# Weighted sum of two expert outputs: the first load in one piece, and the zeroes made by ScalarE

## The chip, the cores and the metric

The kernel runs on one core of one Trainium2 chip. The metric is the device time of one execution in microseconds; the median of three runs of the kernel before is 238.86 us (238.84 to 238.90).

## The reference

```python
expert_outputs   # (16, 1024, 2, 512) float32
combine_weights  # (16, 1024, 2)      float32
weights = combine_weights[..., np.newaxis]
return np.sum(expert_outputs * weights, axis=2).astype(np.float32)   # (16, 1024, 512)
```

There are 16 x 1024 = 16,384 tokens. Each has two expert outputs of 512 numbers and two weights; the output is the weighted sum of the two. The input is twice as large as the output.

## The kernel before

**Layout.** The tokens are spread over 128 partitions, 128 tokens to a partition. One token's input, both experts, is 4 KB (`k * h` = 1024 floats). The first 115 tokens of a partition (`main`) come from one part of the input, the last 13 (`LAST`) from another, so that the last tile has rows of its own. `TILES` (line 32) cuts the 128 tokens into ten tiles of 12 or 13; a tile of 13 is 13 x 4 KB = 52 KB in each partition.

**Rooms.** The buffer `et` (line 62) has four rooms (`ROOM`, line 29) of 13, 13, 12 and 13 tokens. Tile g goes into room g mod 4. A tile is combined in place, and its result, half as large, is stored out of the same room (the last tile's result goes into room 0, by `FREE`). So the load of tile g + 4 has to wait for the store of tile g.

**The work of one tile** (`combine`, line 81). For tiles 0 to 7 VectorE multiplies the whole tile by its weights (line 88) and adds the two halves (line 97). Tile 8 is shared between ScalarE (line 92) and VectorE (lines 94 to 97). For tile 9 ScalarE multiplies one half of each token (line 102), and VectorE multiplies the other and adds (line 103), token by token.

**Queues.** Loads are issued by SyncE (line 76), and so are the last two stores (line 130: tiles 7 and 8 together, and tile 9). All other stores, and the weights, are issued by ScalarE. The order on each engine is the order of the program; nothing reorders it. An instruction that waits holds up what stands behind it on its engine.

**The start.** VectorE clears `zt`, a tile of 16 x 128 floats (line 108). ScalarE then issues its first four DMAs: `zt` to 16 places of the output (line 111; 8 KB, which the true results overwrite later; the first store waits for it), the weights of the first 115 tokens of each partition (line 112, through line 79; 128 rows of 920 bytes into `wt`), and the weights of the last 13 in two halves (line 114). After these, an activation of one column (line 115, into `warm`) has ScalarE load its activation table. SyncE meanwhile issues five loads (lines 118 and 119): `FIRST` (line 33) splits tile 0 into 2 and 11 tokens, and the 2 are moved in pieces of at most 4 KB (`max_dma_last_dim`), one token each; the 11 and the tiles 1, 2 and 3 go as one row of 44, 52, 48 and 52 KB for each partition.

**Counters.** Each DMA counts up a semaphore when it lands. There are eight of them, given out by the framework, so DMAs share them, and one that takes a counter over waits until the DMA that had it has landed.

Of the kernel before, what the change touches and what calls it, by code (L numbers as in the profile page):

```python
# [1 line left out]

# [4 lines left out]


@with_exitstack
def kernel(  # L10
    ctx: ExitStack,
    tc: tile.TileContext,
    expert_outputs: bass.AP,
    combine_weights: bass.AP,
    out: bass.AP,
):

    nc = tc.nc
    b, s, k, h = expert_outputs.shape
    assert k == 2
    n = b * s
    P = nc.NUM_PARTITIONS
    per = n // P
    assert per * P == n

    ROOM = [13, 13, 12, 13]
    ROOMS = len(ROOM)  # L30
    SITE = [sum(ROOM[:i]) for i in range(ROOMS)]
    TILES = [13, 13, 12, 13, 13, 13, 12, 13, 13, 13]
    FIRST = [2, 11, 13, 12, 13]
    STORES = [[0], [1], [2], [3], [4], [5], [6], [7, 8], [9]]
    WHOLE = [0, 1, 2, 3, 4, 5, 6, 7]
    MIXED = [8]
    ALONE = 3
    FREE = {9: 0}
    LAST = 13
    assert all(c <= ROOM[g % ROOMS] for g, c in enumerate(TILES))  # L40
    assert sum(TILES) == per and [g for st in STORES for g in st] == list(range(len(TILES)))
    main = per - LAST
    starts = [sum(TILES[:g]) for g in range(len(TILES))]

    def rows(x):

        first = x[0 : P * main, :].rearrange("(p t) f -> p t f", p=P)
        second = x[P * main : n, :].rearrange("(p t) f -> p t f", p=P)
        return lambda t, c: first[:, t : t + c, :] if t < main else second[:, t - main : t - main + c, :]

    flat = out.rearrange("b s h -> (b s) h")
    eo = rows(expert_outputs.rearrange("b s k h -> (b s) (k h)"))
    cw = rows(combine_weights.rearrange("b s k -> (b s) k"))
    o = rows(flat)

    dt = mybir.dt.float32
    mult = mybir.AluOpType.mult
    add = mybir.AluOpType.add
    copy = mybir.ActivationFunctionType.Copy

    pool = ctx.enter_context(tc.tile_pool(name="all", bufs=1))
    et = pool.tile([P, sum(ROOM), k * h], dt)
    halves = et.rearrange("p j (k h) -> p (j k) h", k=k)
    wt = pool.tile([P, per * k], dt)
    wk = wt.rearrange("p (t k) -> p t k", k=k)
    zt = pool.tile([16, 128], dt)
    warm = pool.tile([P, 1], dt)

    def place(t):
        g = max(g for g in range(len(TILES)) if starts[g] <= t)  # L70
        return SITE[g % ROOMS] + t - starts[g]

    def load(t, c, **kw):
        at = place(t)
        assert place(t + c - 1) == at + c - 1
        nc.sync.dma_start(out=et[:, at : at + c], in_=eo(t, c), **kw)  # L76

    def weights(q, t, c):
        q.dma_start(out=wk[:, t : t + c, :], in_=cw(t, c))

    def combine(g, base):
        at, c, t0 = SITE[g % ROOMS], TILES[g], starts[g]
        if g in WHOLE or g in MIXED:
            room = halves[:, k * at : k * (at + c), :]
            x0, x1 = et[:, at : at + c, 0:h], et[:, at : at + c, h : 2 * h]
            if g in WHOLE:
                wb = wt[:, k * t0 : k * (t0 + c)].unsqueeze(2).to_broadcast([P, k * c, h])
                nc.vector.tensor_tensor(out=room, in0=room, in1=wb, op=mult)  # L88
            else:
                for i in range(ALONE, c):  # L90
                    x = et[:, at + i, 0:h]
                    nc.scalar.activation(out=x, in_=x, func=copy, scale=wt[:, k * (t0 + i) : k * (t0 + i) + 1])  # L92
                w1 = wk[:, t0 : t0 + c, 1:2].to_broadcast([P, c, h])
                nc.vector.tensor_tensor(out=x1, in0=x1, in1=w1, op=mult)  # L94
                w0 = wk[:, t0 : t0 + ALONE, 0:1].to_broadcast([P, ALONE, h])
                nc.vector.tensor_tensor(out=x0[:, 0:ALONE], in0=x0[:, 0:ALONE], in1=w0, op=mult)  # L96
            nc.vector.tensor_tensor(out=halves[:, base : base + c, :], in0=x0, in1=x1, op=add)  # L97
            return
        for i in range(c):
            t = k * (t0 + i)  # L100
            x0, x1 = halves[:, k * (at + i), :], halves[:, k * (at + i) + 1, :]
            nc.scalar.activation(out=x0, in_=x0, func=copy, scale=wt[:, t : t + 1])  # L102
            nc.vector.scalar_tensor_tensor(  # L103
                out=halves[:, base + i, :], in0=x1, scalar=wt[:, t + 1 : t + 2], in1=x0, op0=mult, op1=add
            )

    with tc.manual_schedule():
        nc.vector.memset(zt, 0.0)  # L108

        ahead = flat[0 : P * main, :].rearrange("(q t) h -> q (t h)", q=16)  # L110
        nc.scalar.dma_start(out=ahead[:, 0:128], in_=zt)  # L111
        weights(nc.scalar, 0, main)
        for half in (slice(0, P // 2), slice(P // 2, P)):
            nc.scalar.dma_start(out=wk[half, main:per, :], in_=cw(main, per - main)[half])
        nc.scalar.activation(out=warm, in_=nc.const_aps.tensor(1.0, (P, 1), dt), func=copy)  # L115

        t = 0
        for i, c in enumerate(FIRST):
            load(t, c, **({"max_dma_last_dim": k * h * 4} if i == 0 else {}))
            t += c  # L120
        assert t == sum(TILES[:ROOMS])
        for j, st in enumerate(STORES):
            room = FREE.get(st[0], st[0] % ROOMS)
            base, c = SITE[room] * k, 0
            for g in st:
                combine(g, base + c)
                c += TILES[g]
            assert c <= k * ROOM[room]
            q = nc.sync if j in (7, 8) else nc.scalar
            q.dma_start(out=o(starts[st[0]], c), in_=halves[:, base : base + c, :])  # L130
            for g in st:
                if g + ROOMS < len(TILES):
                    load(starts[g + ROOMS], TILES[g + ROOMS])


# [1 line left out]
_INS = ['expert_outputs', 'combine_weights']  # L137
_OUTS = [((16, 1024, 512), 'float32')]


# [23 lines left out]
```

## Time and profile before

| what | value |
|---|---|
| median of three runs | 238.86 us |
| span of the profiled execution, first to last instruction | 237.1 us |
| VectorE busy | 190.0 us |
| ScalarE busy | 15.8 us |
| moved by DMA | 100.80 MB (67.24 read, 33.56 written) |
| mean rate over the span | 425 GB/s |

The profile is of one execution. It gives that execution's span and not its device time; the difference of the span to the median of the runs is 1.76 us. Times in the rows are microseconds from the start of the span, durations marked ns are nanoseconds. Each row of the timeline has its start, its length, the engine, the line of the kernel, the operation, the tile written and read, and in brackets the idle time before it and what ended that idle time. An engine name that ends in q (SPq, ACTq) is the engine's instruction queue issuing a DMA; the rows of DMA issues give the size of each DMA and the median time from issue to landing. The rows of stages give a stretch of time, its length, the busy time of VectorE (DVE), ScalarE (ACT) and GpSimd (POOL) with the number of instructions that touch it, the granted clock of the matmul engine, which this kernel doesn't use, then the mean share of the 16 DMA engines that is busy, and the rate.

### The profile page before, as it was taken

How to read it: one execution, taken by the hardware profiler on the slowest of the kernel's cores; microseconds unless marked ns; L12 is line 12 of the kernel's file. 1: busy time of each engine (PE TensorE's matmuls, PEld its weight loads, DVE VectorE, ACT ScalarE, POOL GpSimd, SP SyncE). 2: the span in 40 equal slices, each digit the busy share in tenths (PEclk: the TensorE clock that was granted, in tenths of full speed). 3: DMA queues.
4: the chain of work that ended last, by engine and by line, in shares of the span. 5: the costliest groups of instructions: out<-in, count | busy, mean ns of one | idle time of the engine just before them, and what ended most of it. 6: DMA issues, size and time to landing. Idle time of an engine off the chain costs nothing.

```text
span 237.1 us, 154 instructions
## 1 busy us (share of the span) xinstructions
DVE 190.0 (80%) x33; ACT 15.8 (7%) x25; POOL 0.2 (0%) x4
## 2 busy tenths in 40 slices
DVE  0006999999999999999999998998499969919400
ACT  2000000000000000000000000000000055019200
POOL 0000000000000000000000000000000000000000
DMA  8999999989999999999899999999899999899996
GB/s 300 388 481 434 432 421 398 470 348 485 449 431 458 431 440 390 486 420 420 359 492 409 409 509 392 431 503 431 359 431 503 420 397 483 381 431 431 431 431 287
DMA packets 3344, 100.80 MB, mean 425 GB/s; under 512 B 512, under 2 KB 656, under 8 KB 912
## 3 DMA queue, kind: packets, MB, share of 16 engines
q1 hardware_dynamic: 2000, 77.33, 75.9%
q10 hardware_dynamic: 1344, 23.47, 23.0%
HBM read 67.24 MB, written 33.56 MB: 425 GB/s over the span
## 4 chain that ended last, share of the span: by engine, by line
DVE 55%; DMA 36%; issue 1%; ACT 0%; DVEq 0%; ACTq 0%; SPq 0%
DVE et L88 35%; DVE et L97 17%; DMA out_dram<-et 17%; DMA et<-in_expert_outputs_dram 12%; DMA wt<-in_combine_weights_dram 8%; DVE et L103 3%; ACT et L102 0%; DVEq L159 0%; ACTq L111 0%; DVE zt L108 0%; DVEq L88 0%; SPq L76 0%; ACTq L102 0%
## 5 line engine op out<-in xcount | busy, mean ns | idle before, releaser
L88 DVE TENSOR_TENSOR et<-et,wt 128x13312 f32<-128x13312 f32 (+1 forms) x8 | 110.0, 13754 | 23.8 <-DMA wt<-in_combine_weights_dram 18.7
L97 DVE TENSOR_TENSOR et<-et 128x6656 f32<-128x6656 f32 (+1 forms) x9 | 62.8, 6973 | 0.4
L92 ACT ACTIVATE et<-et,wt 128x512 f32<-128x512 f32 x10 | 6.2, 708 | 188.0 <-DMA et<-in_expert_outputs_dram 188.0
L103 DVE SCALAR_TENSOR_TENSOR et<-et,wt 128x512 f32<-128x512 f32 x13 | 8.7, 747 | 5.0 <-ACT et L102 5.0
L102 ACT ACTIVATE et<-et,wt 128x512 f32<-128x512 f32 x13 | 8.1, 707 | 14.0 <-DMA et<-in_expert_outputs_dram 14.0
L94 DVE TENSOR_TENSOR et<-et,wt 128x6656 f32<-128x6656 f32 x1 | 7.1, 7093 | 2.3 <-DMA et<-in_expert_outputs_dram 2.3
L96 DVE TENSOR_TENSOR et<-et,wt 128x1536 f32<-128x1536 f32 x1 | 1.8, 1751 | 0.0
L115 ACT ACT_TABLE_LOAD x1 | 1.3, 1283 | 3.1 <-issue 3.1
L108 DVE MEMSET zt<- 16x128 f32 x1 | 0.2, 165 | 0.8 <-PEq L148 0.8
L115 ACT ACTIVATE warm<-const-float32-1.0 128x1 f32<-128x1 f32 x1 | 0.2, 203 | 0.0
L148 POOL MEMSET const-bfloat16-1.0<- 128x1 bf16 x1 | 0.1, 102 | 0.0
L148 POOL MEMSET const-uint8-127<- 128x1 uint8 x1 | 0.1, 101 | 0.0
L148 POOL MEMSET const-float32-0.0<- 128x1 f32 x1 | 0.1, 99 | 0.2 <-issue 0.2
L148 POOL MEMSET const-float32-1.0<- 128x1 f32 x1 | 0.1, 98 | 0.0
## 6 DMA issues: line engine op xcount, KB each, us to landing
et<-in_expert_outputs_dram SPq DMA_DIRECT2D x7, 6656.0 KB, 32.2
out_dram<-et ACTq DMA_DIRECT2D x5, 3328.0 KB, 34.7
et<-in_expert_outputs_dram SPq DMA_DIRECT2D x2, 6144.0 KB, 41.1
out_dram<-et SPq DMA_DIRECT2D x1, 6656.0 KB, 19.9
out_dram<-et ACTq DMA_DIRECT2D x2, 3072.0 KB, 37.2
et<-in_expert_outputs_dram SPq DMA_DIRECT2D x1, 5632.0 KB, 18.2
out_dram<-et SPq DMA_DIRECT2D x1, 3328.0 KB, 14.0
et<-in_expert_outputs_dram SPq DMA_DIRECT2D x1, 1024.0 KB, 5.0
```

Source lines behind the costliest of these rows:

```text
L88: nc.vector.tensor_tensor(out=room, in0=room, in1=wb, op=mult)
L92: nc.scalar.activation(out=x, in_=x, func=copy, scale=wt[:, k * (t0 + i) : k * (t0 + i) + 1])
L94: nc.vector.tensor_tensor(out=x1, in0=x1, in1=w1, op=mult)
L96: nc.vector.tensor_tensor(out=x0[:, 0:ALONE], in0=x0[:, 0:ALONE], in1=w0, op=mult)
L97: nc.vector.tensor_tensor(out=halves[:, base : base + c, :], in0=x0, in1=x1, op=add)
L102: nc.scalar.activation(out=x0, in_=x0, func=copy, scale=wt[:, t : t + 1])
L103: nc.vector.scalar_tensor_tensor(out=halves[:, base + i, :], in0=x1, scalar=wt[:, t + 1 : t + 2], in1=x0, op0=mult, op1=add)
L108: nc.vector.memset(zt, 0.0)
L115: nc.scalar.activation(out=warm, in_=nc.const_aps.tensor(1.0, (P, 1), dt), func=copy)
L148: nc = _bacc.Bacc("TRN2", target_bir_lowering=False, num_devices=1)
```

## The change

Three things differ. `FIRST` has four entries in place of five, so tile 0 is loaded by one DMA with one row of 52 KB for each partition, and the limit of 4 KB for a piece is gone. The zeroes are written by a ScalarE activation (a copy of the constant 0.0) in place of VectorE's memset. That activation stands first on ScalarE, so the activation table is loaded ahead of it, and ScalarE's four first DMAs stand behind it; the activation of `warm` behind them is dropped, with its tile.

```diff
-    FIRST = [2, 11, 13, 12, 13]
+    FIRST = [13, 13, 12, 13]
...
-    warm = pool.tile([P, 1], dt)
...
-    def load(t, c, **kw):
+    def load(t, c):
         at = place(t)
         assert place(t + c - 1) == at + c - 1
-        nc.sync.dma_start(out=et[:, at : at + c], in_=eo(t, c), **kw)
+        nc.sync.dma_start(out=et[:, at : at + c], in_=eo(t, c))
...
     with tc.manual_schedule():
-        nc.vector.memset(zt, 0.0)
-
+        nc.scalar.activation(out=zt, in_=nc.const_aps.tensor(0.0, (16, 128), dt), func=copy)
         ahead = flat[0 : P * main, :].rearrange("(q t) h -> q (t h)", q=16)
         nc.scalar.dma_start(out=ahead[:, 0:128], in_=zt)
         weights(nc.scalar, 0, main)
         for half in (slice(0, P // 2), slice(P // 2, P)):
             nc.scalar.dma_start(out=wk[half, main:per, :], in_=cw(main, per - main)[half])
-        nc.scalar.activation(out=warm, in_=nc.const_aps.tensor(1.0, (P, 1), dt), func=copy)
 
         t = 0
-        for i, c in enumerate(FIRST):
-            load(t, c, **({"max_dma_last_dim": k * h * 4} if i == 0 else {}))
+        for c in FIRST:
+            load(t, c)
             t += c
```

## The prediction

> **What bounds the kernel now.** I read the page first, then the busy time by stage, then the timeline at both ends.
>
> ```profile
> span 237.1 us, 154 instructions
> DVE 190.0 (80%) x33; ACT 15.8 (7%) x25; POOL 0.2 (0%) x4
> DMA  8999999989999999999899999999899999899996
> DMA packets 3344, 100.80 MB, mean 425 GB/s; under 512 B 512, under 2 KB 656, under 8 KB 912
> ```
>
> VectorE is busy for 80% of the span. The DMA row matters more: the 16 DMA engines stand at eight or nine tenths in every slice but the last. The stages, with the columns length, DVE, ACT, POOL, clock, DMA share, GB/s:
>
> ```profile
> 0.00:19.73 19.73, 0.17 (x2) 1.49 (x2) 0.20 (x4) 1.00 0.96 395
> 19.73:41.00 21.27, 21.23 (x3) 0.00 (x0) 0.00 (x0) 1.00 1.00 429
> 41.00:100.00 59.00, 58.90 (x6) 0.00 (x0) 0.00 (x0) 1.00 0.99 427
> 100.00:208.60 108.60, 101.00 (x12) 6.23 (x10) 0.00 (x0) 1.00 1.01 439
> 208.60:222.30 13.70, 8.71 (x13) 8.07 (x13) 0.00 (x0) 1.00 1.01 435
> 222.30:236.00 13.70, 0.00 (x0) 0.00 (x0) 0.00 (x0) 1.00 0.86 373
> ```
>
> From 19.73 to 222.3 the share is 0.99 to 1.01, so the engines hold no reserve (a packet counts in the window in which it begins, which is why a share can pass 1 and why the last window looks low). The kernel is its 100.80 MB at some 430 GB/s, plus the start and the last receipt. A change can move the end in two ways only: it changes how soon or how fast the first bytes flow, or it makes VectorE so late that the DMA engines run dry. The time, 238.86 us, is 1.76 us above the profiled span of 237.1; that execution's own time is not shown apart, so I take 1.76 as what lies around the span, and leave it as it is.
>
> **The start, as it is.**
>
> ```profile
> 0.73 4.52 SPq L76 DMA_DIRECT2D et<-in_expert_outputs_dram  x5
> 0.81 0.17 DVE L108 MEMSET zt<- 16x128 f32 x1 [0.81 <-PEq L148]
> 1.01 0.39 ACTq L111 DMA_DIRECT2D out_dram<-zt  x1
> 1.43 0.45 ACTq L79 DMA_DIRECT2D wt<-in_combine_weights_dram  x1
> 1.91 1.16 ACTq L114 DMA_DIRECT2D wt<-in_combine_weights_dram  x2
> 3.09 1.28 ACT L115 ACT_TABLE_LOAD   x1 [3.09 <-issue]
> 4.39 0.20 ACT L115 ACTIVATE warm<-const-float32-1.0 128x1 f32<-128x1 f32 x1
> 19.73 14.02 DVE L88 TENSOR_TENSOR et<-et,wt 128x13312 f32<-128x13312 f32 x1 [18.75 <-DMA wt<-in_combine_weights_dram]
> ```
> ```profile
> et<-in_expert_outputs_dram SPq DMA_DIRECT2D x1, 5632.0 KB, 18.2
> ...
> et<-in_expert_outputs_dram SPq DMA_DIRECT2D x1, 1024.0 KB, 5.0
> wt<-in_combine_weights_dram ACTq DMA_DIRECT2D x1, 115.0 KB, 18.2
> ```
>
> The weights are 0.12 MB, yet they take 18.2 us from issue to landing, as long as the 5,632 KB load beside them: their rows go through the same engines by turns with the load's rows. VectorE's first multiply waits for them.
>
> **Part 1: the first load becomes one DMA of 52 KB rows.** It replaces 1,024 KB in 4 KB pieces and 5,632 KB in 44 KB rows. What the 4 KB pieces cost shows in fine windows, beside a stretch of loads alone with long rows:
>
> ```profile
> 1.75:2.00 0.25, 0.00 (x0) 0.00 (x0) 0.00 (x0) 1.00 1.60 180
> 2.00:2.25 0.25, 0.00 (x0) 0.00 (x0) 0.00 (x0) 1.00 1.41 147
> 2.25:2.50 0.25, 0.00 (x0) 0.00 (x0) 0.00 (x0) 1.00 0.28 33
> 2.50:2.75 0.25, 0.00 (x0) 0.00 (x0) 0.00 (x0) 1.00 0.52 131
> 2.75:3.00 0.25, 0.00 (x0) 0.00 (x0) 0.00 (x0) 1.00 0.75 262
> ...
> 3.50:4.00 0.50, 0.00 (x0) 0.50 (x1) 0.00 (x0) 1.00 0.99 410
> ```
> ```profile
> 26.00:34.00 8.00, 7.96 (x2) 0.00 (x0) 0.00 (x0) 1.00 0.99 427
> ```
>
> Rate: 1,024 KB is 1.05 MB; at 410 GB/s it takes 2.56 us, at 427 it takes 2.46. Gain 0.10 us. The Trainium skill, "DMA: Bandwidth & Descriptors", section "Why small descriptors are slow", gives each packet about 3 bus cycles on top of one per 32 bytes; for 4 KB that is 3 in 131, so by the page the gain would be 0.06 us, less than the 410 against 427 measured here.
>
> Start-up: from 1.75 to 3.00 the five windows move 0.25 x (180 + 147 + 33 + 131 + 262) = 188 KB, where 427 GB/s would move 534; the missing 346 KB are worth 0.81 us. Part of it is the first answer of the memory, which a 52 KB row waits for too. Part is the dip at 2.25 to 2.75 (33 and 131 GB/s), worth 0.25 x (1 - 33/427) + 0.25 x (1 - 131/427) = 0.40 us; it goes if pieces of 4 KB run out before the next are ready, and stays if it is the memory's own delay. No row decides. From below the bound is a gain of 0.81 (no start-up loss left), from above a loss of 1.2 (each engine stands a whole 52 KB row, 2.0 us, in place of 0.8). I take a gain of 0.15, between nothing and the dip, nearer to nothing, because the first answer has to be waited for either way. The first bytes at 1.75 follow SyncE's issue at 0.73, which nothing moves: 0.
>
> Issues: SyncE issues four loads in place of five before its first wait on a store. A saved issue is at most 4.52/5 = 0.9 us of SyncE with its wait in it, and nothing queued behind it was late: 0. The instruction order of the two programs shows one thing that the diff doesn't: the load of tile 3, which shared a DMA counter with the zero store, now shares one with the first load, and waits for that to land.
>
> ```profile
> SPq L76 <- DMA out_dram<-zt: 2.1, 1, 2.1
> ```
>
> So that load goes out at some 19 us, where the first load's bytes end, in place of about 5 (0.73 + 4.52 ends the five issues). Its cover is the loads of tiles 1 and 2: 25 rows a partition, where 13 are 1,024 + 5,632 KB, so 13.1 MB or 30.7 us at 427 GB/s, queued ahead of it until about 50. Behind it on SyncE stands only the load of tile 4, which waits for a store until 67.8 (below). Cost 0; without the cover it would be up to 14 us.
>
> **Part 2: ScalarE makes the zeroes, its DMAs wait.** VectorE loses a 0.17 us memset that ended 18.7 us before its next work: 0. On ScalarE the table load and the activation come first: beginning at about 0.75 (SyncE and VectorE begin at 0.73 and 0.81), 1.28 + 0.02 + 0.20 ends near 2.3; the wider tile (128 columns in place of 1) adds 0.2 at most, by the row of line 102 below (8.07 us for 13 of 512 columns, 0.62 each). Then 0.39 for the zero store's issue, and the weights' issue begins at 2.7 in place of 1.43. Its last two weight DMAs follow, and ScalarE's next DMA is the first store at 40.9: ScalarE itself has time.
>
> When do the weights land? Two microseconds of the trace, packets by queue, q1 being SyncE's and q10 ScalarE's:
>
> ```profile
> q1 hardware_dynamic: 16, 0.72, 83.2%
> q10 hardware_dynamic: 16, 0.01, 2.1%
> ```
>
> In 8 to 10 us each of the 16 engines began one load row and one weight row: they alternate one to one. 128 weight rows are 8 an engine, so the weights take 8 load rows. Before: a 44 KB row is 5.77 MB / 427 GB/s / 8 = 1.69 us, 8 are 13.5; the other 4.7 of the 18.2 are the way there, the zero store and what stood ahead. After: a 52 KB row is 2.0 us, 8 are 16.0. Landing at 2.7 + 4.7 + 16.0 = 23.4, so VectorE starts 3.7 us later. Bounds: 1.3 (the issue's shift alone) to 5.7 (one more row, for the zero store's own turn).
>
> Does that reach the end? VectorE's waits later on, and what is late next:
>
> ```profile
> 145.69 12.96 DVE L88 TENSOR_TENSOR et<-et,wt 128x12288 f32<-128x12288 f32 x1 [1.10 <-DMA et<-in_expert_outputs_dram]
> ...
> 169.18 14.03 DVE L88 TENSOR_TENSOR et<-et,wt 128x13312 f32<-128x13312 f32 x1 [3.94 <-DMA et<-in_expert_outputs_dram]
> ...
> 192.63 7.09 DVE L94 TENSOR_TENSOR et<-et,wt 128x6656 f32<-128x6656 f32 x1 [2.30 <-DMA et<-in_expert_outputs_dram]
> ...
> 208.61 14.02 SPq L130 DMA_DIRECT2D out_dram<-et  x2
> 212.80 8.07 ACT L102 ACTIVATE et<-et,wt 128x512 f32<-128x512 f32 x13 [13.95 <-DMA et<-in_expert_outputs_dram]
> ```
> ```profile
> 67.80 116.45 SPq L76 DMA_DIRECT2D et<-in_expert_outputs_dram  x6
> ```
> ```profile
> DMA to landing us min/median/max: 5.0/31.9/71.7
> ```
>
> VectorE waits 1.10 + 3.94 + 2.30 = 7.3 us for loads before tile 8 begins. A start 3.7 late (5.7 at most) is swallowed there, and tile 8 still begins when its load lands. On the way the stores leave 3.7 later, and each load into a freed room is issued later. The first of these went out at 67.80, while the load before it, issued just before 5.25, landed 71.7 us later (the longest in the row below it), near 76.7: 9 us of cover, more than 3.7. Meanwhile the engines, not sharing with stores yet, get further with the loads; the bytes are the same. Cost 0. If the cover were gone, VectorE's delay would reach the store issued at 208.61. That store must be there before the last load lands, by 212.8 where ScalarE's wait ends, less 1.0 from issue to first bytes (0.73 to 1.75): 3.2 us more. So the start may slip by 7.3 + 3.2 = 10.5 us before the engines stand still, and beyond that the end moves one for one.
>
> **The sum.** 237.1 - 0.10 (rate) - 0.15 (start-up) + 0 + 0 = 236.85; with 1.76 around it, 238.6 us.
>
> **The rivals.**
> *Start-up shrinks more.* The dip goes wholly and the first answer is shorter too: 0.40 to 0.81 plus 0.10, so 237.95 to 238.36, say 238.2. For it: the dip of 33 GB/s. Against it: the first windows run at 147 to 180 with all pieces queued, so it is the memory that answers slowly.
>
> *The first rows stall (slower).* At the start each engine has one 52 KB row in hand, and if its slow first answer holds the whole row, the slowest engine stays behind to the end, as all get equal shares. Price up to 1.2 - 0.10, so 239.96 at most, 239.5 midway; it decides from 0.6 us of extra loss on. Against it: later rows run at 427 GB/s without a gap.
>
> *The weights starve (slower).* If an engine finished a whole load before it turned to the other queue, the zeroes would go after the first load and the weights after the second, at some 19 + 16 = 35: 15.3 late, 4.8 over the 10.5. That gives 238.6 + 4.8 = 243.4. Against it stands the alternation of 16 and 16 packets. The Trainium skill, "DMA: Bandwidth & Descriptors", section "Queues, rings and completion order", says that an engine drains a whole packet, typically 9 to 17 descriptors, from one ring before it switches, which for 8 rows and a completion would be one load; by that rule this rival is what happens, and the trace's one-to-one turns speak against it.
>
> *Nothing happens:* the gains are lost in the same start-up, 238.86; it lies within the forecast's case.
>
> **How the numbers follow.** A measurement of this kernel tells about 0.2%, 0.48 us, from no change. Forecast, with nothing, 0.50 (238.4 to 239.3, the same); start-up shrinks 0.29 (faster); first rows stall 0.13 and weights starve 0.08 (both slower). The range 237.9 to 239.9 leaves out the starved weights and about 0.1 at the two edges. Faster 0.29, same 0.50, slower 0.21.
>
> **What would show it.** Right: first bytes near 1.75; 4 KB packets gone; the table load near 0.75 and the weights issued near 2.7; VectorE's first multiply at 21 to 25.5; its waits before tiles 6, 7 and 8 smaller by what the start lost; the tile 3 load issued near 19; the last load landing at 212 to 213; DMA shares of 0.99 to 1.01 until 222. Wrong: a slice with a dip below eight tenths in mid-span, a first multiply after 30, or a start-up loss far from 0.8 us.

## The result, and the profile after

The changed kernel takes 242.61 us (median of 5 runs, 242.11 to 243.68) against 238.86 us: 1.0165 times as long, with an interval of 1.0151 to 1.0179. It is slower by 3.75 us, and outside the range of the prediction. The profiled execution is the longest of the five, 243.68 us: its span is 4.8 us above the profiled one of the kernel before (241.9 against 237.1), where the medians differ by 3.75.

The head of its page, with busy time and the DMA row in 40 slices:

```profile
span 241.9 us, 151 instructions
DVE 189.8 (78%) x32; ACT 15.9 (7%) x25; POOL 0.2 (0%) x4
DMA  7999999999999999999999999999999999979993
```

VectorE does the same work in the same time. Behind the first slice, two things in the DMA row are new: a slice of seven tenths near the end, the 36th, and a last slice of three tenths. The timeline of the start:

```profile
0.73 1.28 ACT L107 ACT_TABLE_LOAD   x1 [0.73 <-PEq L145]
2.02 0.31 ACT L107 ACTIVATE zt<-const-float32-0.0 16x128 f32<-16x128 f32 x1
2.36 0.39 ACTq L109 DMA_DIRECT2D out_dram<-zt  x1
2.78 0.45 ACTq L78 DMA_DIRECT2D wt<-in_combine_weights_dram  x1
25.87 14.03 DVE L87 TENSOR_TENSOR et<-et,wt 128x13312 f32<-128x13312 f32 x1 [25.87 <-DMA wt<-in_combine_weights_dram]
```

ScalarE does what was forecast, to a tenth: the weights are issued at 2.78. But they land 23.0 us later, and VectorE begins at 25.87, 6.1 us later than before. The late waits, from the timeline:

```profile
151.36 12.96 DVE L87 TENSOR_TENSOR et<-et,wt 128x12288 f32<-128x12288 f32 x1 [0.63 <-DMA et<-in_expert_outputs_dram]
...
174.87 14.03 DVE L87 TENSOR_TENSOR et<-et,wt 128x13312 f32<-128x13312 f32 x1 [3.96 <-DMA et<-in_expert_outputs_dram]
...
198.15 7.09 DVE L93 TENSOR_TENSOR et<-et,wt 128x6656 f32<-128x6656 f32 x1 [2.12 <-DMA et<-in_expert_outputs_dram]
...
214.13 13.22 SPq L127 DMA_DIRECT2D out_dram<-et  x2
```

The waits that were to swallow the late start are still there: 0.63 + 3.96 + 2.12 = 6.7 us, where they were 7.3. The loads that VectorE waits for have become late with it, each by about 5.6 us (198.15 against 192.63), and the last but one store goes out at 214.13 in place of 208.61. Now the windows of the last part (length, DVE, ACT, POOL, clock, DMA share, GB/s):

```profile
208.60:222.30 13.70, 9.53 (x8) 4.78 (x8) 0.00 (x0) 1.00 0.87 377
...
237.00:238.00 1.00, 0.00 (x0) 0.00 (x0) 0.00 (x0) 1.00 0.99 426
238.00:239.00 1.00, 0.00 (x0) 0.00 (x0) 0.00 (x0) 1.00 0.07 27
239.00:240.00 1.00, 0.00 (x0) 0.00 (x0) 0.00 (x0) 1.00 0.06 27
```

Around 214 the engines stand still for a while (0.87, 377 GB/s), waiting for that store; by the packets of the trace it is 1.3 us in the mean over the 16. Then they run at the full rate until 238, and for two microseconds more at 27 GB/s. A sixteenth of 430 is 27: **one engine of the 16 is still at work**, two rows of 26 KB behind the other fifteen. In the kernel before the end is sharp:

```profile
234.00:235.00 1.00, 0.00 (x0) 0.00 (x0) 0.00 (x0) 1.00 1.05 453
235.00:236.00 1.00, 0.00 (x0) 0.00 (x0) 0.00 (x0) 1.00 0.01 0
```

So some 3 us are lost before the last stretch, and 2 in it, for one engine. The first part begins between 74 and 78. The DMA queues of the changed kernel show it (packets, MB, share of 16 engines; q1 is SyncE's, q10 ScalarE's):

```profile
q10 hardware_dynamic: 70, 1.84, 106.4%
q1 hardware_dynamic: 1, 0.00, 0.0%
```

SyncE's queue of loads is empty. In the same window of the kernel before, loads and stores shared the engines evenly:

```profile
q1 hardware_dynamic: 32, 0.85, 49.4%
q10 hardware_dynamic: 32, 0.85, 49.4%
```

In these 4 us themselves nothing is lost: the stores alone move 1.84 MB, where loads and stores together moved 1.70. The loss comes when the loads are back (first the changed kernel, then the kernel before):

```profile
84.00:96.00 12.00, 12.00 (x2) 0.00 (x0) 0.00 (x0) 1.00 0.96 371
```
```profile
84.00:96.00 12.00, 11.97 (x2) 0.00 (x0) 0.00 (x0) 1.00 0.97 421
```

The engines are as busy as before, but their rows take longer. By the packets of the traces a load row of 52 KB takes 1.97 us in both kernels as a rule; of the 240 that the changed kernel begins between 60 and 110, 46 take over 0.1 us more, up to 3.06 us, and in the kernel before none of 272 does. Why the rows of loads that come back are slow is not shown.

The queue was empty because the load of tile 4 had to wait for the store of tile 0, and that was late:

```profile
76.02 0.33 SPq L75 DMA_DIRECT2D et<-in_expert_outputs_dram  x1
```

### The profile page after: what moved, and what is told of

It reads as the page before. It is cut to its first block, busy times and chain, and to the rows that moved or that the text cites. A ratio compares the mean times of both kernels' runs of the same rounds, so it can differ in the third digit from the quotient of the medians.

```text
span 241.9 us, 151 instructions
## 1 busy us (share of the span) xinstructions
DVE 189.8 (78%) x32; ACT 15.9 (7%) x25; POOL 0.2 (0%) x4
## 4 chain that ended last, share of the span: by engine, by line
DVE 52%; DMA 37%; issue 3%; ACT 1%; DVEq 0%; ACTq 0%; SPq 0%
DVE et L87 34%; DMA out_dram<-et 15%; DVE et L96 14%; DMA et<-in_expert_outputs_dram 13%; DMA wt<-in_combine_weights_dram 10%; DVE et L102 3%; ACT L107 1%; ACT et L101 0%; DVEq L156 0%; ACTq L109 0%; ACT zt L107 0%; SPq L75 0%; DVEq L87 0%; ACTq L101 0%
```

## Experiments

Each kernel was timed against the kernel before on the same chip. "Start" below is the start of VectorE's first multiply of a tile.

### First round: each part alone, and a late VectorE alone

`load_alone`: the kernel before with the first part of the change.

```diff
-    FIRST = [2, 11, 13, 12, 13]
+    FIRST = [13, 13, 12, 13]
...
-            load(t, c, **({"max_dma_last_dim": k * h * 4} if i == 0 else {}))
+            load(t, c)
```

> Part 1 alone: tile 0 in one DMA of 52 KB rows, the zeroes still by VectorE's memset. Late-start theory (VectorE's late start uses up the 9 us by which the load of tile 4 was issued ahead of need): what counts is when VectorE begins; with the weights issued at 1.43 I expect the first multiply at 22 to 24.5, and a time of 238.8 to 240.5, between the two kernels. Out-of-step theory (long first rows set the 16 engines apart, and each landing waits for the slowest): nearly the whole loss, 241.5 to 243, whatever VectorE's start.

242.56 us (1.0154, 1.0138 to 1.0169): all of the loss, as the two parts together take 242.61. But the start was at 26.06, not at 22 to 24.5, so it tells neither theory from the other: the weights were issued at 1.46, 1.3 us earlier than in the changed kernel, and landed no earlier. **The long rows by themselves hold the weights back.**

`zero_alone`: the changed kernel with the first load as before.

```diff
-    FIRST = [13, 13, 12, 13]
+    FIRST = [2, 11, 13, 12, 13]
...
-            load(t, c)
+            load(t, c, **({"max_dma_last_dim": k * h * 4} if i == 0 else {}))
```

> Part 2 alone: zeroes by ScalarE behind its table load, tile 0 still in 2 and 11 tokens with 4 KB pieces. Late-start theory: weights issued at 2.78, first multiply at 21.5 to 24.5, time 238.8 to 240, the queue of loads never empty. Out-of-step theory: the engines start as in the kernel before, so 238.9, and landings of one load stay within 0.5 us of each other.

239.40 us (1.0036, 1.0014 to 1.0058), with two of the ten runs at 241.0 and 241.7. Start at 23.50; the queue of loads never empty. This is the late-start forecast, with a small loss.

`delay3` and `delay6`: the kernel before with n dummy multiplications, 10 and 20.

```diff
+        w = wt[:, 0 : k * main]
+        one = nc.const_aps.tensor(1.0, (P, k * main), dt)
+        for _ in range(n):
+            nc.vector.tensor_tensor(out=w, in0=w, in1=one, op=mult)
         for j, st in enumerate(STORES):
```

> The kernel before, with ten multiplications of the weights by 1.0 on VectorE ahead of its first multiply, some 3 us in all, results unchanged. DMAs at the start as before. Late-start theory: first multiply at about 22.8, cover of 9 us less 4/3 x 3 = 5 left, so no loss: 238.7 to 239.1. Out-of-step theory: 238.9 too.

> The same with twenty multiplications, some 6 us. Late-start theory: first multiply at about 25.8 as in the changed kernel, cover 9 less 4/3 x 6 = 1, less than the 1.0 from issue to first bytes, so SyncE's queue runs empty near 74 and the time is 240.5 to 243. Out-of-step theory: 238.9, since the start of the DMAs is as before. The prediction's own slack of 10.5 us would also say 238.9.

They took longer than meant, 4.30 and 8.63 us in the profile. 241.69 us (1.0124, 1.0107 to 1.0141) with the start at 24.09, and 240.52 us (1.0073, 1.0053 to 1.0093) with the start at 28.23. A late VectorE alone costs up to 2.8 us, with the DMAs of the start untouched, so the prediction's slack of 10.5 us is refuted. But the late-start theory missed `delay3`, and the longer delay costs less than the shorter.

### Second round: early weights behind long rows, and more delays

`w_act`: the changed kernel with the weights first on ScalarE.

```diff
+        weights(nc.scalar, 0, main)
         nc.scalar.activation(out=zt, in_=nc.const_aps.tensor(0.0, (16, 128), dt), func=copy)
...
         nc.scalar.dma_start(out=ahead[:, 0:128], in_=zt)
-        weights(nc.scalar, 0, main)
```

`w_sync`: the same with `weights(nc.sync, 0, main)`, so that they stand ahead of the first load.

> The changed kernel with the weights' big DMA issued first on ScalarE, ahead of the activation and the zero store; 52 KB rows for tile 0 as in the changed kernel. Empty-queue theory (the loss comes when VectorE starts so late that SyncE's queue of loads runs empty near 74 and the store of tile 0 lands after the load of tile 3): the weights join two or more rows earlier, first multiply at 19.5 to 22, queue never empty, 238.4 to 239.5. Rows-out-of-step theory (the 52 KB rows at the start set the engines apart by 1.1 us and that is the loss): 241.5 to 243 as before.

> The changed kernel with the weights' big DMA issued by SyncE ahead of the first load, all else as in the changed kernel (zeroes by ScalarE, 52 KB rows). Empty-queue theory: the weights land within 4 us, the first multiply waits for the first load alone and starts at 19.5 to 20, time 238.4 to 239.2. Rows-out-of-step theory: 241.5 to 243.

240.99 us (1.0088, 1.0073 to 1.0103) and 240.58 us (1.0076, 1.0061 to 1.0091). The starts are at 20.00 and 20.47, the load of tile 4 goes out at 69.61 and 70.92, and no queue runs empty. So the empty queue is not the whole loss: **1.7 to 2.1 us remain with VectorE in time**. The end of `w_act`:

```profile
235.20:236.20 1.00, 0.00 (x0) 0.00 (x0) 0.00 (x0) 1.00 0.07 27
236.20:237.20 1.00, 0.00 (x0) 0.00 (x0) 0.00 (x0) 1.00 0.06 27
```

All but one of the engines begin their last row by 235.2, about as in the kernel before; one engine alone needs two rows more. The rows-out-of-step theory has the right mechanism, but only about half of the loss that it forecast.

`delay2` and `delay14`: 5 and 14 dummy multiplications.

> The kernel before with five multiplications of the weights by 1.0, 2.15 us by the 0.43 us each that ten took, results unchanged: first multiply at 21.9. Empty-queue theory: cover is 9 less 4/3 x 2.2 = 6, no loss, 238.7 to 239.2. A theory that any late start costs in proportion (2.8 us for 4.3): 240.3.

> The same with fourteen, 6.0 us: first multiply at 25.8, as in the changed kernel, but with the engines in step at the start (landings of the first loads within 0.5 us). Empty-queue theory: queue of loads empty near 74, 240.3 to 242.5. Rows-out-of-step theory: it needs the 52 KB rows at the start, so 238.9 to 239.5.

238.89 us (1.0003, 0.9981 to 1.0026) with the start at 21.49, and 241.52 us (1.0116, 1.0099 to 1.0133) with the start at 25.43. Two microseconds are free. Six cost 2.7 us, with the engines in step at the start (first landings within 0.4 us). Of the 2.7 us, 0.4 lie outside the span: device time and span differ by 2.2 us in all four runs of `delay14`, and by 1.7 to 1.8 in those of the kernel before. Why is not known. Between 74 and 78 `delay14` shows stores alone, and as many bytes as the kernel before:

```profile
q10 hardware_dynamic: 65, 1.70, 99.6%
```

Between 41 and 100 it moves 416 GB/s, where the kernel before moved 427: 59 us x 11 GB/s is 0.65 MB, 1.5 us of work not done. Here too rows take longer: 31 of the 237 load rows of 52 KB begun between 60 and 110 by over 0.1 us, up to 3.26 us.

```profile
41.00:100.00 59.00, 58.93 (x6) 0.00 (x0) 0.00 (x0) 1.00 1.01 416
```

### Third round: the length of the first rows

`pieces4k` and `pieces26k`: the changed kernel, its one DMA for tile 0 cut into pieces of 4 and of 26 KB (`k * h * 4` and `k * h * 4 * 13 // 2`).

```diff
-            load(t, c)
+            load(t, c, **({"max_dma_last_dim": k * h * 4} if i == 0 else {}))
```

`split8k`: the kernel before without the limit, so that its first two tokens go as one row of 8 KB. `zero_w`: `zero_alone` with the weights moved as in `w_act`.

> The changed kernel, its one DMA for tile 0 cut into 4 KB pieces, all else as in the changed kernel. Two-losses theory (long first rows set the engines apart by about 1 us, some 2 us at the end; and weights that wait behind long rows start VectorE late, some 2 us more): both gone, as the engines begin in step (first load's landings within 0.5 us) and the weights take turns with 4 KB pieces, so VectorE starts near 20; time 238.8 to 239.6. Late-start theory alone: the same. If the one DMA by itself, and not its row length, costs: above 240.5.

> The same with 26 KB pieces. Weights' eight turns cost 1 us each, so VectorE starts near 20 in any case. Two-losses theory: the first rows still wait for a cold first answer, so the spread of the first load's landings is 0.5 to 1.1 us and the time 239.5 to 241, as with the early weights. Late-start theory alone: 238.9.

> The kernel before without the 4 KB limit: tile 0 still as 2 and 11 tokens, the 2 as rows of 8 KB. Two-losses theory: the first answer is shared by 8 rows for each engine in place of 16, spread of the first landings 0.3 to 0.8 us, VectorE at 19.7 to 22, time 238.9 to 240. Late-start theory alone: 238.9 as long as VectorE starts before 23.7.

> Part 2 alone with the weights' big DMA ahead of the activation: tile 0 in 2 and 11 tokens with 4 KB pieces, zeroes by ScalarE. Engines in step and weights early: VectorE at 19.5 to 20.5, stores' landings within 0.6 us of each other in place of the 2.2 that part 2 alone has, time 238.7 to 239.1. If ScalarE's zeroes cost by themselves: 239.4 as in part 2 alone.

| kernel | first rows | start | us | ratio and interval |
|---|---|---|---|---|
| `pieces4k` | 4 KB, all of tile 0 | 20.59 | 239.83 | 1.0037 (1.0024 to 1.0050) |
| `pieces26k` | 26 KB | 20.00 | 240.85 | 1.0081 (1.0066 to 1.0096) |
| `split8k` | 8 KB, then 44 KB | 19.30 | 238.79 | 0.9995 (0.9986 to 1.0004) |
| `zero_w` | 4 KB, then 44 KB | 19.93 | 239.47 | 1.0036 (1.0014 to 1.0057) |

With 4 KB pieces the one DMA comes within 0.95 us of the kernel before, a little over its forecast; its trace shows 411 GB/s from 4 to 18 us, and 6.8 MB at 410 in place of 427 GB/s is 0.66 us of it. At 26 KB VectorE starts in time and the loss is that of `w_act`: row length, not the weights, is what is left. Rows of 8 KB are as good as 4 KB. `zero_w` missed: its ten runs lie from 238.93 to 240.81, four of them at 240.8 and the others at 239.7 or below. Its profiled run is one of those four, and ends like the changed kernel's, one engine alone for two rows:

```profile
235.00:236.00 1.00, 0.00 (x0) 0.00 (x0) 0.00 (x0) 1.00 0.07 27
236.00:237.00 1.00, 0.00 (x0) 0.00 (x0) 0.00 (x0) 1.00 0.06 27
```

### Fourth round: one engine behind, and the edge of the late start

`lag_one`: the kernel before with 52 KB more for one engine at the start.

```diff
+        at = SITE[3]
+        nc.sync.dma_start(out=et[0:1, at : at + 13], in_=eo(starts[3], 13)[0:1])
         t = 0
         for i, c in enumerate(FIRST):
```

> The kernel before, with one DMA more at the very start: 52 KB into one partition of the room of tile 3 (the data that tile 3's load brings there anyway, so results are unchanged), some 2 us of work for one engine. Straggler theory (an engine that is 2 us behind at the start stays behind, every landing waits for it, and the last store ends with it alone): first landings 2 us apart, the last stretch at 27 GB/s, a sixteenth, time 240.6 to 241.3. If lag is made up by the queues: 239.0, by 0.12 us of extra work shared by 16.

240.56 us (1.0081, 1.0064 to 1.0098). The start is at 21.54, which `delay2` showed to be free. The load of tile 4 goes out at 72.27, 6.3 us before the load of tile 3 has landed, so no queue runs empty. The straggler theory holds: one engine's 2 us at the start are 1.7 us of the kernel's time. The last rows, of the longest of the four runs (241.46 us):

```profile
236.00:237.00 1.00, 0.00 (x0) 0.00 (x0) 0.00 (x0) 1.00 0.13 53
237.00:238.00 1.00, 0.00 (x0) 0.00 (x0) 0.00 (x0) 1.00 0.06 27
```

`delay8`: eight dummy multiplications. `fix8k`: `zero_w` with the 8 KB rows of `split8k`. `nozero8k`: `split8k` without the zeroes and their store.

> The kernel before with eight multiplications of the weights, 3.4 us, first multiply near 22.9. Empty-queue theory: the edge lies between 23.5 (part 2 alone, queue not empty, 239.4) and 24.1 (ten multiplications, 241.7), so 238.8 to 239.5 here, and the load of tile 4 issued 1 to 4 us before the load of tile 3 lands. Proportional theory: 241.2 or so, four fifths of the loss of ten.

> The changed kernel with both losses taken out: weights' big DMA first on ScalarE, tile 0 as 2 and 11 tokens with 8 KB rows for the 2, zeroes still by ScalarE. Two-losses theory: engines in step and VectorE at 19.3 to 20, time 238.7 to 239.2. If ScalarE's late zero store among long rows sets the engines apart by itself: 239.4 to 241, scattered as with 4 KB pieces.

> The kernel before with 8 KB rows and without the zeroes and their store (the true results are written to those places anyway). Straggler theory: nothing sets the engines apart, 238.6 to 239.0. If the early store keeps the engines in step when the true stores join near 46: landings after 50 more than 1 us apart, 239.5 to 241.

`delay8`: 239.92 us (1.0045, 1.0030 to 1.0060) with the start at 22.92, more than the empty-queue theory allowed and less than proportional. As in `delay14`, 2.2 us lie outside the span in each of its runs; in the span it loses 0.6 us. `fix8k`: 240.03 us (1.0052, 1.0022 to 1.0082), three of its six runs at 238.9 to 239.3 and three at 240.7 to 240.8. `nozero8k`: 239.94 us (1.0045, 1.0018 to 1.0072), five of ten runs at 238.7 to 239.2 and five at 240.7 to 241.0. In both the profiled run is one of the short ones, whose last engine is done 0.7 and 0.5 us after the first. Both missed their forecast of a single value. What is common to them and `zero_w` is that the two groups lie 1.6 to 2 us apart, two rows of 26 KB; that the longer runs are those with a straggler is shown for `zero_w` alone. `zero_alone` and `delay2` have such runs too, two and one of ten. None of the three kernels is faster than the kernel before.

### How far apart the engines are

The traces also have the time at which each of the 16 engines ended its share of a DMA. The table has the distance between the first and the last engine, at the load that completes tile 0 and at the last store, and how much longer the profiled span is than the 237.1 us of the kernel before, all in us:

| kernel | apart at tile 0 | apart at the last store | first engine done | span longer by |
|---|---|---|---|---|
| before | 0.4 | 0.4 | 236.0 | 0 |
| `split8k` | 0.4 | 0.3 | 235.9 | -0.1 |
| `nozero8k` | 0.6 | 0.5 | 235.9 | 0.2 |
| `fix8k` | 0.6 | 0.7 | 235.8 | 0.3 |
| `pieces4k` | 0.8 | 0.8 | 236.2 | 0.8 |
| `zero_w` | 0.8 | 2.2 | 236.0 | 1.9 |
| `pieces26k` | 1.0 | 2.1 | 236.1 | 2.0 |
| `w_act` | 1.1 | 2.4 | 235.9 | 2.1 |
| `w_sync` | 1.3 | 1.4 | 236.3 | 1.6 |
| `lag_one` | 2.2 | 2.5 | 236.4 | 2.6 |

The first engine is done at nearly the same time in all of them, and the loss is nearly the lateness of the last one. In `w_act` the engines are 1.1 us apart up to 41, while loads run alone, and 2.2 apart at the store that lands at 69.5, after the stores have joined the loads. The changed kernel is 1.1 apart at tile 0 and 2.0 at the last store.

### What the delays have in common

Ordered by VectorE's start the losses make no sense. They do, roughly, by the lead with which the load of tile 4 was issued before the load of tile 3 had landed (issue from the timeline; landing as last issue of the first loads plus the longest time to landing). The last column is the median of the spans less 237.1 us:

| kernel | start | tile 4's load issued | tile 3's load landed | lead | loss, us | loss in the span |
|---|---|---|---|---|---|---|
| before | 19.73 | 67.80 | 76.6 | 8.8 | 0 | 0 |
| `delay2` | 21.49 | 69.72 | 75.6 | 5.9 | 0 | 0 |
| `zero_alone` | 23.50 | 72.25 | 75.2 | 3.0 | 0.5 | 0.5 |
| `delay8` | 22.92 | 72.36 | 75.3 | 2.9 | 1.1 | 0.6 |
| `delay3` | 24.09 | 74.98 | 75.1 | 0.1 | 2.8 | 2.8 |
| `delay14` | 25.43 | 74.50 | 74.2 | none | 2.7 | 2.2 |
| `delay6` | 28.23 | 74.09 | 73.0 | none | 1.6 | 1.6 |
| after | 25.87 | 76.02 | 75.8 | none | 3.8 | 3.7 |

In the span a lead of 6 us costs nothing, 3 us about half a microsecond, and none 1.6 to 2.8; the changed kernel has the long rows on top. `w_act` and `w_sync`, with leads of 9.1 and 7.2 us, lose 2.1 and 1.7 all the same: that is the part of the long first rows. The lead shrank by 1.6 to 2.0 us for each microsecond of delay in `delay2`, `delay8` and `delay3`, and not by the 4/3 of the forecasts, which is why `delay3` was missed. Why `delay6`, the latest start, costs less than `delay14` was not settled.

## Why the prediction was wrong, step by step

**What bounds the kernel: right.** The DMA engines hold the time: by the packets of the trace all 16 are at work from 20 to 204 in the changed kernel too. What it loses there it loses in rows that take longer.

**Rate and issues: right, and small.** The first bytes flow between 1.50 and 1.75, no later than before, and the table load, activation and issues came at the times given. A gain from the start-up is not to be seen.

**The load of tile 3: right.** It went out at 19.75, held by the first load, with two loads ahead of it. In `w_act` it is as late (20.0), in `w_sync` it goes out at 2.9, and the two kernels differ by 0.4 us in all.

**When the weights land: too early.** The term "2.7 + 4.7 + 16.0 = 23.4" measured 25.87, outside its own bounds of 1.3 to 5.7 us (6.1). `load_alone` shows that the 1.3 us of ScalarE's wait were not the cause: with 52 KB rows the weights land at the same time when they are issued at 1.46. The way ahead of the eight turns, 4.7 us, was taken over from a start with 4 KB pieces; behind long rows it is longer. The zero store, ahead of the weights in ScalarE's queue, takes 7.3 us from issue to landing in place of 3.9. It lands at 2.36 + 7.3 = 9.7. Eight rows of 2.0 us after that make 25.7, and the weights landed at 25.8.

**"The start may slip by 10.5 us": wrong, and the step that failed most.** In the span `delay8` loses 0.6 us at 3.2 us of delay, and `delay3` 2.8 at 4.4. VectorE's waits for loads were counted as slack, but a wait ends when a load lands, and the load starts when a store of VectorE's own result has landed. A late start moves both ends of the wait. The cover that was counted, 9 us at the load of tile 4, was the true limit. It shrinks from both sides, as the store of tile 0 comes later and the loads ahead run out sooner: from 8.8 to 5.9 for 1.8 us of delay, and to 0.1 for 4.4. "Mixed order, same bytes, cost 0" failed too: once the queue of loads has run dry, rows of the loads that come back take up to 3.06 us in place of 1.97, the engines move less though they never stop (416 GB/s in place of 427 in `delay14`), and the loads stay late to the end. The wait for the last but one store comes on top in some: 1.3 us in the changed kernel's profiled run, 0.5 in `load_alone`, none in `delay14`.

**"The first rows stall": the right mechanism, priced and weighted too low.** It was given 239.5 and a chance of 0.13. `w_act`, `w_sync` and `pieces26k` put it at 1.7 to 2.1 us, about half of the loss, and `lag_one` shows that an engine that is behind at the start is behind at the end. The price went by the mean over the engines; the time goes by the last one, and its distance of about 1.1 us at the start grew to 2.2 in `w_act` when the stores joined.

**The weights starve: refuted.** They landed at 25.8 and not at 35, by turns with the first rows of the second load.

The two losses nearly add up: 1.7 to 2.1 for the rows and 2.2, in the span, for the delay of `delay14` are 3.9 to 4.3, a little over the 3.75 measured.

**Left open.** Why one engine falls behind after long first rows, and less after 4 or 8 KB; why its distance grows when the stores join; why load rows take longer after their queue was empty (in `delay3`, whose queue ran dry too, only 6 of 252 do, so these rows are not all of that loss); and why `zero_w`, `fix8k` and `nozero8k` fall into two groups. In `w_sync` the weights go through the engines ahead of the first long rows and it happens all the same, so it is not only the first access of all.

## What to carry to other kernels

Where every transfer is cut evenly over 16 engines, the last engine sets each landing: read the rate in the last microseconds, where a sixteenth of the full rate means one straggler, and begin with short rows (4 or 8 KB here, which did not keep every run of `zero_w`, `fix8k` and `nozero8k` free of the loss). An engine's wait for a load is slack only if that load doesn't itself depend on the engine; in a ring of buffers follow the loop load, compute, store, load, and count the lead with which each load is issued ahead of its queue running dry. A small transfer that shares engines with long rows pays one long row for each of its own, so small and urgent data go ahead of the long rows.

## What was not expected of the hardware

An engine that was 2 us late at the start did not make it up: 52 KB more for one engine cost `lag_one` 1.7 us after 236 us of full queues. And a queue that never runs empty is worth more than its bytes: with the same bytes to move and the engines at work all along, a gap of some 4 us in the loads at 74 cost `delay14` 2.2 us in the span, much of it in load rows that took up to 3.26 us in place of 1.97.
